# A fixed order of TensorE products, more reordered stretches, an fp32r second norm, a shared last multiplication and ten more low parts by accumulating transfers

## The chip, the core and the metric

The program runs on one core of a Trainium2 chip. A core has a matrix engine (PE; its weight loads are listed apart as PEld), a vector engine (DVE), an activation engine (ACT), a general engine (POOL), a sequencer that issues most transfers (SP), and sixteen DMA engines that move data between HBM and the on-chip memory. Each engine works through its own queue in order and waits on semaphores for the others. The metric is the time of one execution in microseconds (us) on the device, taken as the median of several runs.

## The reference: what is computed

Two request groups share all weights: one prompt of 256 tokens and 8 sequences of 4 new tokens, 288 columns in all. One layer is applied, then a last norm:

```python
def trunk_layer(x, ...):
    h = rmsnorm(x, norm1_g)
    proj = jnp.einsum("btd,de->bte", h, w_in) + b_in          # 2048 -> 3072
    a, gate, z = proj[..., :D_CONV], proj[..., D_CONV:2 * D_CONV], proj[..., 2 * D_CONV:]
    u = a * jax.nn.sigmoid(gate)
    c = jax.nn.silu(layernorm(depthwise_causal_conv(u_ext, conv_w, conv_b), ln_g, ln_b))
    d = multiscale_pool(z_ext, pos0)                          # windows 2, 4, 8, 16
    p = jnp.einsum("btgc,gce->btge", d, pool_w).reshape(bsz, T, D_POOL) * pool_scale
    mix = jnp.concatenate([c, p], axis=-1)
    x = x + jnp.einsum("btm,md->btd", mix, w_out)             # 2048 -> 2048
    h2 = rmsnorm(x, norm2_g)
    f = jnp.square(jax.nn.relu(jnp.einsum("btd,df->btf", h2, w_ff1)))   # 2048 -> 8192
    x = x + jnp.einsum("btf,fd->btd", f, w_ff2)               # 8192 -> 2048
    return x, u_ext[:, -(CONV_W - 1):], z_ext[:, -(POOL_MAX - 1):]
```

All arrays are float32. The outputs are the normed x of both groups and the last 30 values of `u` and the last 15 of `z` as new states.

## The kernel before

Channels lie on the 128 partitions, the 288 tokens along the free axis. Every float32 weight and every float32 activation is split into two fp32r numbers, a high part (a rounded copy) and a low part (what is left), and a product of two such numbers is taken as three TensorE products of 128x128 by 128x288: high by high, low weight by high activation, high weight by low activation. They are called products below. There are 8,112 of them and all stand at line 315.

**Weights.** A block is 1024 rows by 256 columns. SP loads it in two raw tiles `wr` of four 128-row slices each (512 KB). ACT casts a raw tile to the high part `whi` (line 265). The low part `wlo` is made in one of three ways (`split_part`, lines 259 to 273): V, DVE subtracts (line 270); G, POOL subtracts in two halves (line 273); D, ACT writes the negated high part into `wlo` (line 267) and POOL issues a transfer that reads the weights from HBM once more and adds them onto `wlo` (line 268). The table `WAYS` (line 73) says which way is taken, by stage, in turn for successive tiles. `whi` and `wlo` have five buffers each, `wr` six; a tile is cast when PE has let go of a buffer, and each tile serves 24 products.

**Stages.** `SEQUENCE` (line 45) gives the order of the input projection: `c0` to `c7` are the eight pairs of 128 channels of `a` and `gate` (96 products each; c0 and c1 are done together), `p3` to `p0` are the four pooling groups (96 each), `P3` to `P0` the products by `pool_w` (12 each). After each pair c, DVE does 30 multiply-adds of the convolution (line 434, `pc`), which keep it full from about 40 to 195 us; POOL does the window sums of each p (lines 466 to 475). `w_out` follows in two halves: first the rows of the pooling channels (`dx` tiles, 8 groups of 48 products, lines 553 to 559), in which between products the mean and the variance of the layer norm are taken, then the rows of the convolution channels (`mx` tiles, 8 groups of 48, lines 576 to 580). In the first half the activations are taken in the order of `korder`, so of a block's two tiles the second is used first. Then come four rounds of 8 groups of `w_ff1` (`ax` tiles, 96 products each) and 8 of `w_ff2` (`fx` tiles, 96 each).

**Order.** Tile, the layer under the kernel, runs its own estimate of the time line and lets an instruction that is ready pass one that is not, in each engine's queue, before the program is built. So the order of products on PE is that of the code only where the estimate sees no wait; `tc.issue_after` pins an order where it is used (lines 231, 314, 508, 555). Inside a group of products `gemm` (line 291) has a list `todo`; `classes`, where given, permutes its head: each product has a class, (k + part of the activation) mod 2, and the string says which class comes next. `TURN` (line 70) is such a string of 48. Without it the classes alternate. `TURN` is used in c2 and in the groups of index 2 of both halves of `w_out` and of the first round of `w_ff1`.

**Norms.** `rsqrt_sums` and `spread` (lines 221 to 251) reduce a row of sums over the partitions with six small float32 products into 96x3 numbers, take the inverse root there, and spread it back with three float32 products. The second norm's row `ss2` is summed up by POOL (line 604) from squares that ACT takes of each finished x (line 603), and is reduced behind the first group of `w_ff1` (line 615). At the end (lines 649 to 653) DVE multiplies the 16 rows of x by the last norm's row in six pieces, and SP sends each off.

Of the kernel before, what the change touches and what calls it, by code (L numbers as in the profile page):

```python
# [44 lines left out]
SEQUENCE = [(_s[0], int(_s[1])) for _s in "c0 c1 c2 c3 c4 p3 c5 p2 P3 c6 p1 P2 p0 P1 c7 P0".split()]  # L45
# [27 lines left out]
WAYS = {"c2": "GVGV", "c3": "GDGG", "c4": "GDGD", "p3": "GDDG", "c5": "GDGD", "c": "GGGV", "p": "GVVG", "w": "GG", "ff": "VV"}  # L73
# [13 lines left out]
def trunk_kernel(ctx: ExitStack, tc: tile.TileContext, io):  # L87
# [133 lines left out]
    def rsqrt_sums(parts, scale, after=None, busy=(0, 0)):  # L221
# [5 lines left out]
        idle = cvp.tile([P, 512], F32, name=nm("idle"), tag="cv") if sum(busy) else None  # L227
        for n, t in enumerate(parts):
            for j in range(3):
                last = nc.tensor.matmul(pt[:TB, j : j + 1], t[:, j * TB : (j + 1) * TB], ones[:, 0:1], start=n + j == 0, stop=n == len(parts) - 1 and j == 2)  # L230
            with tc.issue_after(last.ins):
                for j in range(busy[n] if n < 2 else 0):
                    nc.tensor.matmul(idle[:, 0:P], ones, ones, start=True, stop=True)  # L233
# [12 lines left out]
    def spread(sums):  # L246

        s, pr, _ = sums
        for j in range(3):
            last = nc.tensor.matmul(pr[:, j * TB : (j + 1) * TB], s[:, j : j + 1].to_broadcast([TB, P]), ident, start=j == 0, stop=j == 2)  # L250
        return pr, last

    def rsqrt_rows(*args):
        return spread(rsqrt_sums(*args))[0]

# [34 lines left out]

    def gemm(banks, rhs, m_outer=False, between={}, classes=""):
# [3 lines left out]
        gets = ready.pop()  # L295
        step = 2 if len(banks) == 2 else 1
        pairs = [(k, m) for k in range(0, n, step) for m in range(len(banks))]
        if m_outer:
            pairs.sort(key=lambda km: km[1])
        if step == 2:  # L300
            parts = ((0, 0, 0), (1, 0, 0), (0, 1, 0), (1, 1, 0), (1, 0, 1), (0, 0, 1))
        else:
            parts = ((0, 0, 0), (0, 0, 1), (0, 1, 0))
        todo = [(k + d, m, w, x) for k, m in pairs for d, w, x in parts]
# [407 lines left out]
```

## Time and profile before

| what | us |
|---|---|
| median of 3 runs (lowest, highest) | 1088.29 (1088.22, 1089.59) |
| the profiled execution | 1087.97 |
| its span, from first to last instruction | 1086.2 |
| PE busy | 1073.7 |
| DVE busy | 634.0 |
| ACT busy | 477.9 |
| POOL busy (nearly all of it before 207 us) | 182.7 |

The profiled execution lies 0.3 us under the median and 1.8 us over its own span. Times in the rows below are counted from the first instruction. PE is busy 99% of the span, so what it waits shows only as small gaps; busy time includes a product's own latency (292 ns each, overlapping its neighbours), and the rate at which products start has to be read from a count and the time it takes. In the chain of waits each row gives the start, the length, the engine and tile, and the number of instructions merged; in a time line the bracket at the end of a row tells how long the engine idled before it and what ended that.

### The profile page before, as it was taken

The numbers are of one execution on the slowest core, as the hardware profiler recorded it, in microseconds if no ns is written. First come the engines' busy times: TensorE is split into PE (matmuls) and PEld (weight loads), VectorE is DVE, ScalarE is ACT, GpSimd is POOL, SyncE is SP. The second block draws the span as 40 slices with busy tenths as digits, with TensorE's granted clock in tenths as the row PEclk, the third lists the DMA queues.
The fourth block names the chain that finished last, engine by engine and source line by source line (L and its number), as shares of the span: only waits on it lengthen the run. The fifth ranks groups of instructions, "written<-read, shape, count | busy, mean of one in ns | idle before, by whom it ended". The sixth has DMA issues, their size and how long they took to land.

```text
span 1086.2 us, 19609 instructions
## 1 busy us (share of the span) xinstructions
PE 1073.7 (99%) x8206; PEld 1071.4 (99%) x8206; DVE 634.0 (58%) x813; ACT 477.9 (44%) x583; POOL 182.7 (17%) x212
## 2 busy tenths in 40 slices
PE   9999999999999999999999999999999999999996
PEld 8999999999999999999999999999999999999996
DVE  7899999678555444445454444545544445554553
ACT  8654445475544433334443333444433334444441
POOL 0888989613000000000000000000000000000000
PEclk9999999999999999999999999999999999999998
DMA  9896467545455555555555555555555555555522
GB/s 333 281 269 177 136 178 245 183 153 178 159 171 169 164 172 174 166 167 173 167 167 172 172 165 168 175 167 165 174 169 165 172 173 165 167 174 166 168 76 88
DMA packets 58120, 190.71 MB, mean 176 GB/s; under 512 B 6192, under 2 KB 11312, under 8 KB 58032
## 3 DMA queue, kind: packets, MB, share of 16 engines
q1 hardware_dynamic: 56480, 185.27, 52.2%
q0 software_dynamic: 1008, 3.67, 1.9%
q8 instruction: 64, 1.05, 0.4%
q10 hardware_dynamic: 544, 0.52, 0.1%
q14 instruction: 24, 0.20, 0.0%
HBM read 185.16 MB, written 4.28 MB: 174 GB/s over the span
## 4 chain that ended last, share of the span: by engine, by line
PE 96%; DVE 1%; ACT 1%; DMA 1%; issue 1%; POOL 0%; DVEq 0%
PE ac L315 95%; DMA wr<-in_w 1%; PE pp L315 0%; DVE xT L652 0%; ACT whi L265 0%; DVE wlo L270 0%; POOL wlo L273 0%; PE idle L233 0%; ACT n L567 0%; PE pt L250 0%; PE pt L230 0%; DVE z_all L391 0%; ACT z_all L389 0%; ACT hx L340 0%; DVE n L564 0%
## 5 line engine op out<-in xcount | busy, mean ns | idle before, releaser
L265 ACT CAST whi<-wr 128x1024 fp32r<-128x1024 f32 (+1 forms) x341 | 356.6, 1046 | 558.4 <-PE ac L315 540.4
L270 DVE TENSOR_TENSOR wlo<-wr,whi 128x1024 fp32r<-128x1024 f32 (+1 forms) x295 | 362.9, 1231 | 350.3 <-ACT whi L265 350.3
L315 PE MATMUL ac<-ax,whi 128*128 128x288 f32 x2048 | 351.5, 292 | 0.0
L315 PE MATMUL ac<-fx,whi 128*128 128x288 f32 x2048 | 350.1, 292 | 0.0
L315 PEld LDWEIGHTS ac<-ax,whi 128*128 128x128 f32 x2048 | 296.2, 187 | 0.0
L315 PEld LDWEIGHTS ac<-fx,whi 128*128 128x128 f32 x2048 | 295.6, 187 | 0.0
L315 PE MATMUL ac<-ax,wlo 128*128 128x288 f32 x1024 | 217.4, 292 | 0.0
L315 PE MATMUL ac<-fx,wlo 128*128 128x288 f32 x1024 | 216.3, 292 | 0.0
L315 PEld LDWEIGHTS ac<-ax,wlo 128*128 128x128 f32 x1024 | 162.7, 187 | 0.0
L315 PEld LDWEIGHTS ac<-fx,wlo 128*128 128x128 f32 x1024 | 162.2, 187 | 0.0
L315 PE MATMUL ac<-hx,whi 128*128 128x288 f32 x768 | 136.3, 295 | 0.6 <-DVE hx L338 0.6
L315 PEld LDWEIGHTS ac<-hx,whi 128*128 128x128 f32 x768 | 113.8, 188 | 1.0 <-ACT whi L265 0.8
L273 POOL TENSOR_TENSOR wlo<-wr,whi 128x512 fp32r<-128x512 f32 x78 | 105.9, 1411 | 32.7 <-ACT whi L265 30.4
L434 DVE SCALAR_TENSOR_TENSOR pc<-u_all,vec,pc 128x256 f32<-128x256 f32 x232 | 99.8, 483 | 3.0 <-ACT pc L431 1.6
L315 PE MATMUL ac<-hx,wlo 128*128 128x288 f32 x384 | 86.1, 296 | 0.3 <-DVE wlo L270 0.2
L315 PEld LDWEIGHTS ac<-hx,wlo 128*128 128x128 f32 x384 | 62.7, 188 | 1.1 <-DVE wlo L270 0.9
L315 PE MATMUL ac<-dx,whi 128*128 128x288 f32 x256 | 46.1, 296 | 0.0
L315 PE MATMUL ac<-mx,whi 128*128 128x288 f32 x256 | 45.2, 294 | 0.1
L617 DVE SCALAR_TENSOR_TENSOR t<-ac,r 128x576 f32<-128x576 f32 x32 | 24.2, 758 | 26.3 <-PE ac L315 25.2
L315 PEld LDWEIGHTS ac<-mx,whi 128*128 128x128 f32 x256 | 37.5, 188 | 0.6 <-ACT mx L569 0.3
L315 PEld LDWEIGHTS ac<-dx,whi 128*128 128x128 f32 x256 | 38.0, 188 | 0.1
L646 DVE TENSOR_TENSOR xT<-xT,ac 128x576 f32<-128x576 f32 x24 | 18.1, 754 | 19.4 <-PE ac L315 19.4
(108 smaller groups left out, 502.9 us busy)
## 6 DMA issues: line engine op xcount, KB each, us to landing
wr<-in_w SPq DMA_DIRECT2D x335, 512.0 KB, 3.6
wlo<-in_w POOLq DMA_DIRECT2D x7, 512.0 KB, 7.3
xT<-in_xT SPq DMA_DIRECT2D x7, 288.0 KB, 6.6
out_u_out<-u_all SPq DMA_DIRECT2D x1, 1208.0 KB, 9.7
out_yT<-xT SPq DMA_DIRECT2D x2, 576.0 KB, 2.9
u_all<-in_hist_c SPq DMA_DIRECT2D x8, 136.0 KB, 5.2
wr<-in_w SPq DMA_DIRECT2D x4, 256.0 KB, 3.3
out_z_out<-z_all SPq DMA_DIRECT2D x1, 668.0 KB, 8.2
```

The lines of the kernel that those rows point to most:

```text
L265: nc.scalar.copy(hi, raw)
L270: nc.vector.tensor_tensor(lo, raw, f32(hi), op=ALU.subtract)
L273: nc.gpsimd.tensor_tensor(lo[:, j : j + 2, :], raw[:, j : j + 2, :], f32(hi[:, j : j + 2, :]), op=ALU.subtract)
L315: last = nc.tensor.matmul(banks[m][:, :T], gets[k // 8](k % 8, m)[w], rhs[k][x], start=j == ends[m][0], stop=j == ends[m][1])
L434: nc.vector.scalar_tensor_tensor(out=dst, in0=up[:, w : w + SEQ], scalar=cwv[:, w : w + 1], in1=pc, op0=ALU.mult, op1=ALU.add)
L617: nc.vector.scalar_tensor_tensor(out=t, in0=bk[:, :, :T], scalar=0.0, in1=both(r2), op0=ALU.max, op1=ALU.mult)
L646: nc.vector.tensor_tensor(x2, x2, bk[:, :, :T], op=ALU.add)
```

## The change

- **Order.** Every product from the end of c0/c1 to the third group of `w_ff1` is now issued through `mm`, which pins it behind the product before it (`chain`), so that PE's order is the order of the code there. `gemm` with four banks takes its k in pairs after the first two.
- **Sequence.** P1 is no longer a step of its own: its 12 products stand inside c7, after c7's first 48. P0 follows c7 directly.
- **Repeated reordering.** `TURN` is given to c0/c1, c2, c4 to c7, to groups 1 and 4 of both halves of `w_out`, and to group 1 of the first round of `w_ff1`.
- **Second norm.** The row `ss2` is split into high and low (ACT, DVE) and reduced by two fp32r products with a constant matrix, which also spread it; they stand inside the first group of `w_ff1`, after 24 of its 96 products. Square root, reciprocal and three more DVE operations then run on 128x288.
- **Last norm.** ACT takes the root straight from PSUM, four filler products stand for six, and the last multiplication is shared: DVE takes twelve rows in six pieces, reading the spread row in PSUM, POOL the last four one by one, from a copy that ACT makes. The pieces are sent by SP and ACT in turn.
- **Low parts.** `WAYS` gives way D to one more tile each of c6 and c7 and to the second tile of each of the eight blocks of the first half of `w_out`: ten in all, from G.
- The small load of `vec` goes ahead of the first x.

Three places in the built order, before and after. Names carry the program's numbers.

PE at the start of `w_ff1` (`ac30` is its first group in both; `ss2` the row of squares; `whi85`, `whi86` are that group's first two weight tiles). Before:

```order
L315 MATMUL ac30_3463<-ax7_3449,wlo88_3445 128x288
L315 MATMUL ac30_3463<-ax8_3450,wlo88_3445 128x288
L315 MATMUL ac30_3463<-ax8_3450,whi88_3444 128x288
L315 MATMUL ac30_3463<-ax7_3449,whi88_3444 128x288
L230 MATMUL pt3_3584<-ones_110,ss21_2865 96x1 x3
L315 MATMUL ac31_3606<-ax1_2928,whi89_3564 128x288 x2
```

After:

```order
L303 MATMUL ac30_3490<-ax2_3016,whi85_3371 128x288 x2
L303 MATMUL ac30_3490<-ax2_3016,wlo85_3372 128x288 x2
L303 MATMUL ac30_3490<-ax2_3016,whi85_3371 128x288 x4
L303 MATMUL ac30_3490<-ax2_3016,wlo85_3372 128x288 x2
L303 MATMUL ac30_3490<-ax2_3016,whi85_3371 128x288 x2
L303 MATMUL mean21_3518<-hl_3515,means_157 128x288 x2
L303 MATMUL ac30_3490<-ax3_3089,whi86_3375 128x288 x2
```

The reduction moved from behind the group's 96th product to behind its 24th.

PE at the start of the second half of `w_out` (`mx1` to `mx4` are the four tiles of normed convolution channels, `ac22` and `ac23` the first two groups). Before:

```order
L315 MATMUL ac22_2866<-mx1_2841,whi69_2828 128x288 x2
L315 MATMUL ac22_2866<-mx1_2841,wlo69_2829 128x288 x2
L315 MATMUL ac23_2937<-mx1_2841,whi71_2919 128x288 x2
L315 MATMUL ac23_2937<-mx1_2841,wlo71_2920 128x288 x2
L315 MATMUL ac22_2866<-mx1_2841,whi69_2828 128x288 x4
```

After:

```order
L303 MATMUL ac22_2883<-mx1_2858,whi69_2780 128x288 x2
L303 MATMUL ac22_2883<-mx1_2858,wlo69_2781 128x288 x2
L303 MATMUL ac22_2883<-mx1_2858,whi69_2780 128x288 x4
L303 MATMUL ac22_2883<-mx1_2858,wlo69_2781 128x288 x2
L303 MATMUL ac22_2883<-mx1_2858,whi69_2780 128x288 x2
L303 MATMUL ac22_2883<-mx2_2865,whi69_2780 128x288 x2
```

Before, the two groups alternate, 24 products on each `mx` tile; now the first group runs through all four tiles with 12 products on each before the second begins.

POOL in the first half of `w_out` (`wlo` low parts, `sum_c` the layer norm's sums, `prd8` products of the last convolution pair). Before:

```order
L438 TENSOR_TENSOR prd8_2253<-u_all_87,vec_85 128x8x31 x4
L273 TENSOR_TENSOR wlo58_2416<-wr58_2408,whi58_2415 128x512 x2
L273 TENSOR_TENSOR wlo59_2475<-wr59_2470,whi59_2474 128x512 x2
L443 TENSOR_TENSOR sum_c_242<-sum_c_242,c3_1066 128x288
L273 TENSOR_TENSOR wlo60_2480<-wr60_2472,whi60_2479 128x512 x2
L273 TENSOR_TENSOR wlo61_2539<-wr61_2534,whi61_2538 128x512 x2
```

After:

```order
L456 TENSOR_TENSOR prd8_2272<-u_all_87,vec_85 128x8x31 x4
L275 DMA wlo58_2371<-in_w 128x1024
L280 TENSOR_TENSOR wlo59_2430<-wr59_2425,whi59_2429 128x512 x2
L461 TENSOR_TENSOR sum_c_247<-sum_c_247,c3_1071 128x288
L275 DMA wlo60_2435<-in_w 128x1024
L464 TENSOR_TENSOR sum_c_247<-sum_c_247 128x288
L280 TENSOR_TENSOR wlo61_2494<-wr61_2489,whi61_2493 128x512 x2
```

Every second tile (even numbers, the one that its group uses first) now comes by transfer.

The diff, cut to its core:

```diff
-SEQUENCE = [... "c0 c1 c2 c3 c4 p3 c5 p2 P3 c6 p1 P2 p0 P1 c7 P0".split()]
+SEQUENCE = [... "c0 c1 c2 c3 c4 p3 c5 p2 P3 c6 p1 P2 p0 c7 P1 P0".split()]
+TURNS = ("c4", "c5", "c6", "c7")
...
-WAYS = {... "c": "GGGV", "p": "GVVG", "w": "GG", "ff": "VV"}
+WAYS = {... "c": "GDGV", "p": "GVVG", "w": "GD", "ff": "VV"}
...
+    nc.sync.dma_start(vec[:, 0:NG], io["vec"][:, 0:NG])
     for k, n in FIRST[:6]:
         first_x(k, n)
-        if k == 0:
-            nc.sync.dma_start(vec[:, 0:NG], io["vec"][:, 0:NG])
-        elif k > 1:
+        if k > 1:
             first_weights(k, n, nc.sync)
...
+    def inverse_root(mean, root, y, out):
+
+        nc.vector.reciprocal(y, root)
+        nc.vector.scalar_tensor_tensor(out=root, in0=mean, scalar=EPS, in1=y, op0=ALU.add, op1=ALU.mult)
+        nc.vector.scalar_tensor_tensor(out=root, in0=root, scalar=-0.5, in1=y, op0=ALU.mult, op1=ALU.mult)
+        nc.vector.scalar_tensor_tensor(out=out, in0=root, scalar=1.5, in1=y, op0=ALU.add, op1=ALU.mult)
...
+    chain = []
+
+    def mm(*args, **kw):
+
+        with tc.issue_after(chain[-1]) if chain else nullcontext():
+            last = nc.tensor.matmul(*args, **kw)
+        if chain:
+            chain[0] = last.ins
+        return last
...
-    with tc.issue_after(gemm(pair0 + pair1, hx, between={15: first_sums})):
-        third = conv_products(2, between={2: first_rows}, classes="01" * 18 + TURN)
+    chain.append(gemm(pair0 + pair1, hx, classes="010" * 4 + "101" * 4 + "01" * 24 + TURN))
+    third = conv_products(2, between={0: first_sums, 4: first_rows}, classes="01" * 15 + TURN)
...
+    def pool_between():
+
+        ready.extend(itertools.islice(weights, 1))
+        return pool_products(1)
+
     for kind, i in SEQUENCE[3:]:
         if kind == "c":
-            conv_pair(i, conv_products(i))
+            conv_pair(i, conv_products(i, between={8: pool_between} if i == 7 else {}, classes=TURN if f"c{i}" in TURNS else ""))
...
-        with behind:
-            last = gemm(each(bk), [mixp[k] for k in korder], between=BETWEEN.get(g, {}), classes=TURN if g == 2 else "")
-        behind = tc.issue_after(last) if g > 3 else nullcontext()
+        gemm(each(bk), [mixp[k] for k in korder], between=BETWEEN.get(g, {}), classes=TURN if g in (1, 4) else "")
...
-        gemm(each(bk), mixc, classes=TURN if g == 2 else "")
+        gemm(each(bk), mixc, classes=TURN if g in (1, 4) else "")
...
+    def second_rows():
+
+        hl = actp.tile([P, 4, T], F32R, name="hl", tag="act")
+        hi, lo = hl[:, 1, :], hl[:, 0, :]
+        nc.scalar.copy(hi, ss2)
+        nc.vector.tensor_tensor(lo, ss2, f32(hi), op=ALU.subtract)
+        bk, r2 = ms("mean2"), row("r2")
+        mean, root = bk[:, 0, :T], bk[:, 1, :T]
+        mm(mean, means, hi, start=True, stop=False)
+        last = mm(mean, means, lo, start=False, stop=True)
+        nc.scalar.activation(root, mean, AF.Sqrt, bias=eps)
+        inverse_root(mean, root, r2, r2)
...
-            gemm(each(bk), x1, classes=TURN if ch == 0 and g == 2 else "")
-            if ch == 0 and g == 0:
-                nc.scalar.copy(r2, rsqrt_rows([ss2], 1.0 / D))
+            gemm(each(bk), x1, between={4: second_rows} if ch == 0 and g == 0 else {}, classes=TURN if ch == 0 and g == 1 else "")
+            if ch == 0 and g == 2:
+                chain.clear()
...
-    rf = rsqrt_rows([ssf, qf], 1.0 / D, None, (3, 6))
-    for k0, n in ((0, 1), (1, 2), (3, 4), (7, 4), (11, 3), (14, 2)):
-        xk = xT[:, k0 : k0 + n, :]
-        nc.vector.tensor_tensor(xk, xk, rf[:, None, :T].to_broadcast([P, n, T]), op=ALU.mult)
-        nc.sync.dma_start(io["yT"][:, k0 : k0 + n, :], xk)
...
+    queues = (nc.sync, nc.scalar)
+
+    def finish(eng, r, pieces):
+
+        for j, (k0, n) in enumerate(pieces):
+            xk = xT[:, k0 : k0 + n, :]
+            eng.tensor_tensor(xk, xk, r[:, None, :].to_broadcast([P, n, T]), op=ALU.mult)
+            queues[j % 2].dma_start(io["yT"][:, k0 : k0 + n, :], xk)
+
+    finish(nc.vector, rows_f, ((0, 1), (1, 1), (2, 2), (4, 2), (6, 3), (9, 3)))
+    nc.scalar.copy(rf, rows_f)
+    finish(nc.gpsimd, rf, [(k, 1) for k in range(12, KT)])
```

In the built order ACT's queue ends with the root, three issues of the last DVE pieces (of one, two and three rows), then the copy `rf`, then two issues of POOL's rows. P1's 12 products stand on PE between the 48th and 49th of c7.

More of the change, by code (lines that the diff above doesn't have):

```diff
@@ L309, in gemm @@
         ends = {m: [f(j for j, p in enumerate(todo) if p[1] == m) for f in (min, max)] for m in range(len(banks))}
[L310 removed]
         for j, (k, m, w, x) in enumerate(todo):
[L312 to L315 removed]
+            if begins.get(j) in between:
+                between[begins[j]]()
+            last = mm(banks[m][:, :T], gets[k // 8](k % 8, m)[w], rhs[k][x], start=j == ends[m][0], stop=j == ends[m][1])
         ready.extend(itertools.islice(weights, 1))
@@ L491, in pool_products @@
             mixp[i] = (mh, ml)
+        return last
     for i in range(2):
```

80 lines of the change are left out of this document (48 added, 32 removed).

## The prediction

> **What bounds the kernel now.** First the page's list of engines:
>
> ```profile
> PE 1073.7 (99%) x8206; PEld 1071.4 (99%) x8206; DVE 634.0 (58%) x813; ACT 477.9 (44%) x583; POOL 182.7 (17%) x212
> ```
>
> PE is never idle for long, so the time is the number of products times the distance between their starts, plus the few waits. The distance comes from the table of windows (start and end, length, PE busy with its instructions, granted clock, DMA share, GB/s):
>
> ```profile
> 85.00:109.00 24.00, 24.00 (x182) 1.00 0.59 171
> 242.00:270.00 28.00, 28.00 (x218) 1.00 0.55 183
> 310.00:1070.00 760.00, 760.00 (x5849) 1.00 0.50 163
> 1072.00:1086.20 14.20, 3.81 (x35) 0.78 0.42 167
> ```
>
> Some two products already run when a window opens, so I take two from each count: 24.00/180 = 133.3 ns, 28.00/216 = 129.6, 760/5847 = 130.0. There are two gaits at the same full clock, 3.3 ns apart. The chain of waits (start, length, engine and tile) shows how little else there is:
>
> ```profile
> 164.75 1.30 POOL wlo L273
> 166.10 3.71 PE ac L315 x26
> ...
> 220.70 63.42 PE ac L315 x480
> 284.12 0.43 PE pt L230 x6
> ...
> 290.24 0.64 PE pt L250 x6
> 290.88 781.06 PE ac L315 x6006
> ```
>
> The reader is to see that 6,006 of 8,112 products stand in one unbroken run of 781.06 us (130.0 ns each), and that the change touches what lies ahead of it and the end. Every microsecond that PE waits there is lost whole, since nothing later has slack to give it back.
>
> **The change part by part.** Sums go against the profiled execution, 1087.97 us; the median lies 0.3 above it.
>
> *Reordered stretches.* They remove no product. The slow window lies in c5 to p0, the fast ones behind the group that has `TURN` already. If the string brings the fast gait from c5's on, the 456 products from there to p0's end gain 456 x 3.3 ns = 1.5 us. The other new strings lie where the gait is fast already or where I expect waits to break it. The ends are 0 and, for about 1,100 slow products of the front (that window's gait up to the one at 242), -3.6. I take -1.5. The small load placed ahead of the first x I leave at 0 (+-0.3): it is 8 KB.
>
> *P1 inside c7.* Its 12 products now stand 48 products, 6.3 us, behind p0's last. The way to its operands before:
>
> ```profile
> 151.57 0.75 DVE L457 TENSOR_TENSOR tz<-ac,rb 128x576 f32<-128x576 f32 x1
> ...
> 156.89 0.79 POOL L475 TENSOR_TENSOR d<-s,z_all 128x32 f32<-128x32 f32 x1
> ...
> 157.71 0.68 ACT L477 CAST dx<-d 128x576 fp32r<-128x576 f32 x1 [2.33 <-POOL d L475]
> ...
> 159.44 0.75 DVE L478 TENSOR_TENSOR dx<-d,dx 128x576 fp32r<-128x576 f32 x1
> ```
>
> This is the last window sum that P1 and P0 wait for in the row of steps. p0's products end shortly before 151.57, say 151.5; the high part is there 6.9 us later (158.39), the low part 8.7 (160.19), of which DVE spends one on convolution pieces that stand first. PE comes at 6.3 and is served at 7.9 to 8.7: a wait of 1.6 to 2.4. Before, P1 had waited for nothing, but a POOL low part cost some 0.3 there:
>
> ```profile
> L315 PEld LDWEIGHTS ac<-dx,wlo 128*128 128x128 f32 x128 | 20.9, 188 | 0.4 <-POOL wlo L273 0.3
> ```
>
> It goes. Net +1.3 (-0.3 if POOL, relieved of low parts, is early enough; 2.1 at most).
>
> *Ten low parts by transfer.* Each takes POOL's two halves of a subtraction away and adds an ACT pass, a POOL issue and 512 KB of traffic. Rows of the seven that exist, then one cast in the first half of `w_out` and the group end behind which its products come, then the two state outputs and the issue of the larger one:
>
> ```profile
> L268 POOL DMA_DIRECT2D wlo<-in_w x7: 817/875/1169, 42.4 to 83.8; - x7
> ...
> DMA to landing us min/median/max: 5.8/7.3/10.1
> ```
>
> ```profile
> L267 ACT ACTIVATE wlo<-whi 128x1024 fp32r<-128x1024 f32 x7 | 7.4, 1058 | 0.1
> ```
>
> ```profile
> 183.81 1.05 ACT L265 CAST whi<-wr 128x1024 fp32r<-128x1024 f32 x1 [2.29 <-PE ac L315]
> ```
>
> ```profile
> 193.08 0.75 DVE L559 TENSOR_TENSOR xT<-xT,ac 128x576 f32<-128x576 f32 x1 [0.89 <-PE ac L315]
> ```
>
> ```profile
> out_u_out<-u_all SPq DMA_DIRECT2D x1, 1208.0 KB, 9.7
> ...
> out_z_out<-z_all SPq DMA_DIRECT2D x1, 668.0 KB, 8.2
> ```
>
> ```profile
> 172.26 0.55 SPq L522 DMA_DIRECT2D out_u_out<-u_all  x1
> ```
>
> From cast to use lie 193.08 - 183.81 = 9.3 us, and the cast cannot come earlier, since it waits for PE to free a buffer. Needed are 1.05 (cast) + 1.06 (second pass) + 0.3 (an allowance for the semaphores until POOL issues) + 5.8, 7.3 or 10.1 = 8.2, 9.7 or 12.5 us: 1.1 early, 0.4 late or 3.2 late. All eight in `w_out` are the tiles that their group uses first. PE waiting here also holds the casts behind it, so a wait lengthens the next tile's lead; they do not simply add. The state outputs leave ahead of and beside the first groups (the larger at 172.26, one or two tiles before the cast shown) and load the engines more than what stood beside the seven. I price two tiles at half the longest shortfall (3.2), the rest at 0.3 together: +3.5. Ends: 0 (all as the quickest) and eight times 0.4 plus 14.8 from four late ones, 18. The Trainium skill ("DMA: Bandwidth & Descriptors", section on the anatomy of a SWDGE transfer) gives about 2.0 us + bytes/436e3 for such a transfer, by which 512 KB would take an estimated 3.2 us and this term would be 0; the seven rows here, accumulating ones, do not agree (5.8 at least), and the rows decide.
>
> *Second half of w_out.* Its first two groups alternated; now the first alone needs all four `mx` tiles, and the second follows. What feeds the fourth, and the second group's end:
>
> ```profile
> 225.27 1.15 ACT L567 ACTIVATE n<-n,vec 128x288 f32<-128x288 f32 x2
> 226.53 1.06 ACT L265 CAST whi<-wr 128x1024 fp32r<-128x1024 f32 x1
> 227.48 0.67 ACT L569 CAST mx<-n 128x576 fp32r<-128x576 f32 x1
> ```
>
> ```profile
> 228.76 0.76 DVE L570 TENSOR_TENSOR mx<-n,mx 128x576 fp32r<-128x576 f32 x1
> ...
> 234.11 0.75 DVE L580 TENSOR_TENSOR xT<-xT,ac 128x576 f32<-128x576 f32 x1 [0.31 <-PE ac L315]
> ```
>
> The fourth tile is whole at 228.2 and 229.5 (about 228.8 where DVE takes it at once). PE started at 220.70 and has 36 products for the three tiles ahead, done by 225.5 at the soonest: it stands until 228.8, does what is left of the first group by 229.9, and then 48 products x 131 ns, to 236.2. Before, both groups were done 0.2 before 234.11. +2.3; +0.5 if the chain of the norm starts earlier, +3 if the fourth tile comes at 229.5.
>
> *Second norm.* The fp32 pieces of the chain, 0.43 and 0.64, go; two products (0.26) come, after 24 products of the group:
>
> ```profile
> 271.48 0.42 PE L315 MATMUL ac<-ax,whi 128*128 128x288 f32 x2
> ```
>
> ```profile
> 273.64 2.00 POOL L604 TENSOR_TENSOR ss<-ss,q 128x288 f32<-128x288 f32 x2 [4.23 <-ACT q L603]
> ```
>
> ```profile
> 274.80 1.06 ACT L265 CAST whi<-wr 128x1024 fp32r<-128x1024 f32 x1 [0.53 <-PE ac L315]
> ```
>
> ```profile
> 275.89 1.23 DVE L270 TENSOR_TENSOR wlo<-wr,whi 128x1024 fp32r<-128x1024 f32 x1
> ```
>
> ```profile
> L543 DVE TENSOR_TENSOR q<-q 128x288 f32<-128x288 f32 x1 | 0.5, 459 | 0.0
> ...
> L615 ACT COPY r<-pt 128x288 f32<-128x288 f32 x1 | 0.4, 400 | 1.9 <-PE pt L250 1.9
> ```
>
> PE is there at 271.48 + 24 x 0.13 = 274.6. The row of squares is whole at 275.64; ACT's copy follows its cast (275.86 + 0.40 = 276.3), DVE's subtraction its own (277.12 + 0.46, by the row of `q`, = 277.5). PE waits 2.9, and all products are pinned behind. 2.9 + 0.26 - 1.07 = +2.1; +0.7 if ACT and DVE take the row first, +3 if they are late. What comes after the root on 128x288 has the group's other 72 products, 9.4 us, to hide in.
>
> *The end.* ACT sends three of DVE's pieces and waits for each in its queue; its copy for POOL stands behind the last. So POOL's four rows begin after DVE's twelve, not beside them.
>
> ```profile
> 1075.85 5.28 DVE L652 TENSOR_TENSOR xT<-xT,pt 128x288 f32<-128x288 f32 x6 [1.00 <-PE pt L250]
> ```
>
> ```profile
> L604 POOL TENSOR_TENSOR ss<-ss,q x15: 817/911/1732, 235.7 to 274.7; 128x288 f32<-128x288 f32 x15
> ```
>
> ```profile
> 1074.31 0.16 DVE L241 TENSOR_TENSOR st<-st 96x3 f32<-96x3 f32 x1
> ```
>
> ```profile
> 0.72 0.98 ACTq L184 DMA_DIRECT2D wr<-in_w  x2
> ```
>
> ```profile
> DMA to landing us min/median/max: 1.8/2.9/3.8
> ```
>
> DVE's end was 1081.13. Sixteen rows took 5.28, so twelve take 4.1 in as many pieces; two small steps like the one of 0.16, with their hops, fall out of the root (-0.35). DVE is done at 1079.6, then an issue on ACT (0.98 for two, 0.5) and the copy (0.40), and POOL's four rows of 0.82 to 1.0 end at 1083.8 to 1084.5: +3.0. The last transfer was 1 of 2 rows, and is now 1 of 1 row, some 1.6 shorter by the landings of the outputs (1.8 for the one row sent before, up to 3.8). +1.4 (0.7 to 2.3).
>
> Sum: -1.5 + 1.3 + 3.5 + 2.3 + 2.1 + 1.4 = +9.1, so 1087.97 + 9.1 = 1097.1 on the profiled execution, about 1097 as a median too.
>
> **The rivals.** *A, the transfers are in time*, as their quickest row has it: without 3.5, 1093.5. For it, POOL no longer queues anything ahead of the issues; against it, the two outputs. *B, the waits take each other's place.* A later PE finds the convolution, the norm's row and P1 ready, and the string gives all of the front the fast gait: 9.1 less 1.3, 2.3 and 2.1, and 2.1 more gain: 1089, no change. Against it: the second half of `w_out` and the second norm hang on PE's own products, so they move with it. *C, the long run loses its gait.* A wait ahead of `w_ff1` leaves PE at 133.3, and the string of group 1 does not mend it: 6006 x 3.3 = +20 us, 1117. Every fast window here stands behind such a string, so the chance is small. *D, the clock falls behind a wait.* The last window, with PE busy for 3.81 of 14.20 us, has a clock of 0.78, all others 1.00; if each of three waits of 2 to 3 us costs as much again, 1103. The Trainium skill ("TensorE: Matmul & The Clock Gate", Part 1) lets the clock fall after an idle window of about 3.4 us, by which these waits would just not do it; no row here tells. *E, the other side: faster.* The string repeated may bring a third gait, as far under 130.0 as that lies under 133.3: 126.7 ns over the run of 6,006, -20 us, 1077. It decides from (9.1 + 2.2)/6006 = 1.9 ns per product. Against it, the window from 310 to 1070 us is behind such a string already and shows 130.0. The skill's same page (section on the back-to-back gap) has N/2.4 + 2.5 ns, an estimated 122.5 ns for 288 columns, which the trace does not reach. Smaller, on the same side: all terms at their low ends (-3.6, -0.3, 0, 0.5, 0.7, 0.7) give 1086, just past the bound below.
>
> **How the numbers follow.** The forecast has a chance of 0.52, A 0.15, B 0.10, C 0.04, D 0.06, E 0.05, the low ends together 0.08. What a measurement of this kernel can tell from no change is about 0.2%, 2.2 us. Slower: forecast, A, C, D = 0.77; same: B = 0.10; faster: E and the low ends = 0.13. The range leaves out E, most of the low ends and C, and the upper part of the transfers' term: 1087 to 1103. The forecast's own is 1092 to 1103.
>
> **What would show it.** The profile after should have a window of c6 and p0 at 130 ns; a PE gap of 1.6 us ended by DVE `dx` inside c7; gaps ended by the transfers in the first groups of `w_out`, near 180 us; one of 3 us ended by DVE `mx` after 225; one of about 3 ended by DVE's low part of the row of squares 24 products into `w_ff1`; the long run at 130.0; and POOL's four rows behind DVE's twelve. It is wrong if the long run has another gait, if transfers land in over 12 us, or if the gaps are there singly but not together.

## The result, and the profile after

The changed kernel takes 1104.57 us (median of 4 runs, 1103.57 to 1107.27) against 1088.26 before (1087.80 to 1089.59): a ratio of 1.0152, 95% interval 1.0130 to 1.0174. It is 16.3 us slower. Forecast were about 9 us, with a range up to 1103. The sign was right, the size was not, and the time lies outside the range. The profiled execution (1105.53, 1.0 above the median) has a span of 1103.8 us, 17.6 more than before.

First the engines of the changed kernel, then its table of what PE waited for (who waited, for whom, us in total, times, longest):

```profile
PE 1077.5 (98%) x8192; PEld 1072.4 (97%) x8192; DVE 631.5 (57%) x815; ACT 486.4 (44%) x594; POOL 167.5 (15%) x206
```

```profile
PE ac L303 <- DMA wlo<-in_w: 6.9, 4, 3.9
PE mean L303 <- ACT hl L635: 1.5, 1, 1.5
...
PE ac L303 <- ACT mx L591: 0.9, 2, 0.6
PE mean L303 <- DVE hl L636: 0.9, 1, 0.9
PE ac L303 <- DVE mx L592: 0.7, 1, 0.7
```

The largest wait is for low parts that come by transfer. The chain of waits has the three late ones:

```profile
163.65 9.22 DMA wlo<-in_w
...
180.46 8.87 DMA wlo<-in_w
...
195.04 7.83 DMA wlo<-in_w
```

PE starts again as each of them lands (in the bracket, how long it idled):

```profile
172.91 0.53 PE L303 MATMUL ac<-dx,wlo 128*128 128x288 f32 x2 [3.88 <-DMA wlo<-in_w]
...
189.37 0.40 PE L303 MATMUL ac<-dx,wlo 128*128 128x288 f32 x1 [1.95 <-DMA wlo<-in_w]
...
202.91 0.40 PE L303 MATMUL ac<-dx,wlo 128*128 128x288 f32 x1 [0.63 <-DMA wlo<-in_w]
```

The fourth wait of that row of the table, 0.4 us, is for c7's low part by transfer, at 154.7 us.

The windows (start and end, length, PE busy and instructions, granted clock, DMA share, GB/s) show what the waits alone don't:

```profile
140.00:150.00 10.00, 10.00 (x80) 1.00 0.53 154
172.00:182.00 10.00, 9.09 (x57) 0.83 1.08 284
...
290.00:296.00 6.00, 5.89 (x33) 0.72 0.25 87
310.00:1070.00 760.00, 760.00 (x5848) 1.00 0.52 167
```

The long run has the gait it had before (760/5846 = 130.0 ns), and the window at 140 us is fast too. But after the wait that ends at 172.9 us, and after the second norm's two products at 290 us, PE is nearly always busy and does few products: 57 in 10 us. The granted clock is down (a cold clock, below), and products start 240 ns apart instead of 130. In the trace these are 14 products behind the first wait and 11 behind the norm.

To account for the whole, the start of the same product by count is compared in the two traces. Lengths of the stretches, us:

| stretch (numbers of products) | before | after | difference | forecast |
|---|---|---|---|---|
| start, to the 188th | 32.27 | 32.89 | +0.6 | 0 |
| to the 1048th, the gait | 114.57 | 113.46 | -1.1 | -1.5 |
| to the 1201st, c7 with P1 | 20.68 | 22.25 | +1.6 | +1.3 |
| to the 1585th, first half of `w_out` | 53.18 | 62.18 | +9.0 | +3.5 |
| to the 1729th, second half's first groups | 19.58 | 21.99 | +2.4 | +2.3 |
| to the 1969th, the rest of that half | 31.20 | 31.30 | +0.1 | |
| to the 2205th, second norm | 32.25 | 35.60 | +3.4 | +2.1 |
| to the 8112th, the long run | 767.92 | 767.92 | 0.0 | 0 |
| tail, from there to the span's end | 14.55 | 16.21 | +1.7 | +1.4 |

The differences sum to 17.6 before rounding. Each column is one trace: in a second trace of the kernel before (last experiment) the second stretch takes 117.0 us, 2.1 of them a wait for one of its seven transfers at 63 us, and all kernels with the change take 113.5 to 114.0 there.

### The profile page after: what moved, and what is told of

The parts are those of the page before. It is cut to its first block, busy times and chain, and to the rows that moved or that the text cites. A ratio compares the mean times of both kernels' runs of the same rounds, so it can differ in the third digit from the quotient of the medians.

```text
span 1103.8 us, 19604 instructions
## 1 busy us (share of the span) xinstructions
PE 1077.5 (98%) x8192; PEld 1072.4 (97%) x8192; DVE 631.5 (57%) x815; ACT 486.4 (44%) x594; POOL 167.5 (15%) x206
## 4 chain that ended last, share of the span: by engine, by line
PE 69%; issue 21%; DVE 4%; DMA 3%; POOL 2%; ACT 1%; SPq 0%; POOLq 0%; DVEq 0%; ACTq 0%
PE ac L303 68%; DMA wlo<-in_w 2%; DVE pc L452 2%; DMA wr<-in_w 1%; DVE wlo L277 1%; POOL wlo L280 1%; POOL s L484 0%; ACT whi L272 0%; POOL xT L708 0%; ACT n L589 0%; PE pt L303 0%; POOL prd L456 0%; DVE z_all L409 0%; PE pp L303 0%; DVE tz L475 0%
## 5 line engine op out<-in xcount | busy, mean ns | idle before, releaser
L708 POOL TENSOR_TENSOR xT<-xT,rf 128x288 f32<-128x288 f32 x4 | 3.0, 790 | 808.8 <-ACT rf L712 808.8
L280 POOL TENSOR_TENSOR wlo<-wr,whi 128x512 fp32r<-128x512 f32 x58 | 78.9, 1392 | 40.1 <-ACT whi L272 39.3
## 6 DMA issues: line engine op xcount, KB each, us to landing
out_u_out<-u_all SPq DMA_DIRECT2D x1, 1208.0 KB, 12.5
```

Of the source, the lines that this page charges most:

```text
L280: nc.gpsimd.tensor_tensor(lo[:, j : j + 2, :], raw[:, j : j + 2, :], f32(hi[:, j : j + 2, :]), op=ALU.subtract)
L708: eng.tensor_tensor(xk, xk, r[:, None, :].to_broadcast([P, n, T]), op=ALU.mult)
```

## The experiments

Theories: L, every wait counts at its length, since nothing behind it gives time back, and a cold clock behind the longest counts besides. W, the waits only stand in for others. Each edit is against the changed kernel unless another base is named.

### Low parts by subtraction again

```diff
-WAYS = {... "c": "GDGV", "p": "GVVG", "w": "GD", "ff": "VV"}
+WAYS = {... "c": "GDGV", "p": "GVVG", "w": "GG", "ff": "VV"}
```

> The changed kernel with the eight tiles of the first half of w_out subtracted by POOL again (the two more transfers in c6 and c7 stay). Theory L (late transfers, and a cold clock behind the longest of them): the changed kernel's trace has three waits for these transfers, 4.18, 2.24 and 0.92 us from start to start less 0.13 each, together 6.9, and 14 product starts 240 ns apart behind the first, 110 ns each too much, 1.5. Without them the kernel is 8.4 us faster than the changed one, about 1096. Rival W (the waits only stand in for others: the convolution on DVE and the layer norm behind it would be waited for anyway): 3 to 4 us faster at most, about 1101, with a new gap ahead of the second half of w_out.

Measured: 1096.26 us, 8.3 less than the changed kernel. The first half of `w_out` takes 53.07 us, as it did before the change (53.18). W falls: nothing took the place of these waits. The 9.0 us of that stretch belong to the eight transfers.

### The same transfers on the tile used second

```diff
-WAYS = {... "w": "GD", ...}
+WAYS = {... "w": "DG", ...}
```

> The changed kernel with the same number of transfers, but in each block of c6, c7 as they are and of w_out for the other of the two tiles, the one that its group uses second. Theory L: 24 products, 3.1 us, more from cast to use, so that a transfer has some 10 us to land instead of 6.9; with the landings of 7 to 10 us seen, at most 1 us of waits is left: 7 us faster than the changed kernel, about 1097.5. Rival T (the accumulating transfers themselves load the engines until they are late wherever they stand): landings beyond 10 us and gaps of 3 us or more, less than 4 us faster, 1101 or more.

Measured: 1095.70 us, 8.9 less. What PE waits for in this kernel:

```profile
PE mean L303 <- ACT hl L635: 1.5, 1, 1.5
PE ac L303 <- ACT whi L272: 1.2, 1, 1.2
...
PE ac L303 <- DMA wlo<-in_w: 0.3, 1, 0.3
```

Of 6.9 us for transfers 0.3 are left, and these are for c7's low part at 154 us; the eight of `w_out` make PE wait for nothing, with landings no shorter (median 8.5 us). The 1.2 us for ACT's cast lie in the start. So the transfers are not too many or too heavy. They were given to the tile with 24 products less lead.

### The second norm 24 products later

```diff
-            gemm(each(bk), x1, between={4: second_rows} if ...)
+            gemm(each(bk), x1, between={8: second_rows} if ...)
```

> The changed kernel with the second norm's two products after 48 instead of 24 products of the first group of w_ff1. Theory L with the cold clock: the two waits (1.76 and 1.30 us from start to start, less 0.26 of their own) and the 12 starts at 240 ns behind them (1.3) both go: 4.1 us faster than the changed kernel, about 1100.5. Rival N (the slow starts come with the norm itself, not with the wait): 2.8 us faster, and 240 ns intervals behind the two products at their new place. Rival M (the rest of the norm now comes late for the first group's end): a new gap at the second or third group.

Measured: 1100.70 us, 3.9 less. The stretch of the norm takes 31.03 us, 4.6 less than in the changed kernel and 1.2 less than before the change: without the wait the fp32r reduction is the gain that it can be.

This run's trace also has a case of its own in the first half of `w_out`: a wait of 1.90 us with a cold clock behind it.

```profile
188.90 0.40 PE L303 MATMUL ac<-dx,wlo 128*128 128x288 f32 x1 [1.90 <-DMA wlo<-in_w]
```

```profile
189.00:194.00 5.00, 5.00 (x27) 0.66 0.99 262
```

### Useless products in the norm's wait

```diff
+        fill = cvp.tile([P, 512], F32, name="fill", tag="cv")
+        for j in range(6):
+            mm(fill[:, 0:P], ones, ones, start=True, stop=True)
         mm(mean, means, hi, start=True, stop=False)
+        for j in range(4):
+            mm(fill[:, 0:P], ones, ones, start=True, stop=True)
```

> The changed kernel with six float32 products of 128x128 with no use ahead of the second norm's first product and four ahead of its second, so that PE is busy where it waited; the operands come no earlier. Theory L with the cold clock: the waits stay as long as they were, but the 12 starts at 240 ns behind them are 130 ns again: 1.3 us faster than the changed kernel (1.0 to 1.6), about 1103.2. Rival N (the slow starts follow the kind of product, not the idle time): the 240 ns stay, and the time is that of the changed kernel or 0.3 longer.

Measured: 1104.35 us, 0.2 less, which is within the spread of the changed kernel's own runs. The trace decides. The norm's stretch takes 34.16 us instead of 35.60, and PE's window over it stays at full clock:

```profile
284.00:290.00 6.00, 5.87 (x48) 1.00 0.52 175
```

So the slow starts cost 1.4 us in the changed kernel; the waits beside them stayed. The time did not show it, since in this trace 20 products instead of 14 were slow behind the first transfer.

One such trace alone does not show that the useless products did it. Four other traces have the same two waits of the norm, 1.5 and 0.9 us. The changed kernel has 11 slow products behind them, the run with the low parts by subtraction 24 (stretch 36.76 us), and the runs with the tiles exchanged and with the states late (below) none (34.16 us each). So a gap of this length costs a cold clock in one execution and not in another:

```profile
278.00:288.00 10.00, 7.64 (x35) 0.66 0.34 105
```

```profile
278.00:288.00 10.00, 7.63 (x56) 1.00 0.34 105
```

The first is the run with the low parts by subtraction, the second that with the tiles exchanged: PE was busy equally long, with 35 and 56 instructions.

The traces tell what it goes by. In all seventeen the granted clock changes only at whole multiples of 3.413 us from its first change, so each trace falls into stretches of that length. Three of the changed kernel that hold a long wait, each with the stretch behind it:

```profile
170.47:173.88 3.41, 0.96 (x7) 1.00 1.04 344
173.88:177.29 3.41, 3.41 (x16) 0.50 1.05 266
187.53:190.95 3.42, 1.58 (x12) 1.00 1.01 313
190.95:194.36 3.41, 3.41 (x28) 1.00 0.97 252
286.52:289.93 3.41, 1.23 (x8) 1.00 0.50 157
289.93:293.34 3.41, 3.23 (x13) 0.50 0.45 154
```

The views count what runs in a stretch. By the products that start in it, over some 5,300 stretches of the seventeen traces ahead of the tail, half clock came behind each of the eleven with at most 11 starts and behind no other. The wait of 1.95 us at 187 us left 12 starts in its stretch, one of 1.97 us with the states late left 11. So it goes by how much of a gap falls into one stretch, which differs from execution to execution. The norm's stretch of this run:

```profile
286.91:290.32 3.41, 3.28 (x27) 1.00 0.46 154
```

Twenty of its 27 instructions are the useless products (two for each float32 product); without them it would be one of the low ones. This was read off the traces afterwards; no run was made to test it, and 11 and 12 are counts of products of 288 columns in these traces alone.

### Both repairs, as a base

Low parts of the first half of `w_out` by subtraction, and the norm after 48 products, with the edits above.

> The changed kernel with both repairs at once: POOL subtracts the low parts of the first half of w_out, and the second norm's two products stand after 48 products. Theory L: the two gains lie in different places and both are lost time of PE, so they add: 8.3 + 3.9 = 12.2 us faster than the changed kernel, about 1092.4; no product starts at 240 ns behind a wait. Rival: a part of one gain is eaten by a later wait, 1094 to 1096. It serves the next three as their base.

Measured: 1091.74 us, 12.8 less than the changed kernel. The gains add, and the trace has no slow products behind a wait.

### The second half's first groups unpinned (on the base)

```diff
+        if g == 0:
+            chain.clear()
-        gemm(each(bk), mixc, classes=TURN if g in (1, 4) else "")
+        last_m = gemm(each(bk), mixc, classes=TURN if g in (1, 4) else "")
+        if g == 1:
+            chain.append(last_m)
```

> The base of the last run, and the first two groups of the second half of w_out not pinned, so that they alternate again. Theory O (the pinned order costs the difference between standing for the fourth normed tile with 48 products still to do and with few to do): 2.2 us faster than the base, about 1090.2, and the gaps of 0.9, 0.65 and 0.9 us in front of the second to fourth tile are gone or shorter. Rival: the layer norm's own chain on ACT and DVE sets when the tiles come, and the end of the second group is the same: within 0.5 us of the base.

Measured: 1089.34 us, 2.4 less than the base. The two groups alternate again and the stretch takes 19.75 us (base 21.93, before 19.58). The pinned order is the cause.

### The start and P1 (on the base)

```diff
-    nc.sync.dma_start(vec[:, 0:NG], io["vec"][:, 0:NG])
     for k, n in FIRST[:6]:
         first_x(k, n)
-        if k > 1:
+        if k == 0:
+            nc.sync.dma_start(vec[:, 0:NG], io["vec"][:, 0:NG])
+        elif k > 1:
...
-            conv_pair(i, conv_products(i, between={8: pool_between} if ...))
+            conv_pair(i, conv_products(i, between={12: pool_between} if ...))
```

> The base, with two things undone at places that the trace tells apart: the small load of vec behind the first x again, and P1's 12 products inside c7 after 72 products instead of 48. Theory V (the first x comes later because the small load stands ahead of it): the 192nd product starts at 31.3 us instead of 32.4 to 32.8, 1.1 us. Rival R (the new order of the products of c0 and c1 costs it, since it asks for the weights of a pair of rows at once): the 192nd product starts where it did. For P1, theory L: its two waits of 0.4 to 0.8 and 0.65 us go, about 1.0 us; rival: another wait takes their place at P0 or at the first group of w_out. Both theories: 2.1 us faster than the base, about 1090.3.

Measured: 1091.34 us, 0.4 less than the base: neither part did what was expected. The start was no earlier (188th product at 34.61 us in this trace), but this trace cannot judge the load: PE has a cold clock from 12.4 to 15.9 us, so that 14 products start 240 ns apart.

```profile
12.45:15.85 3.40, 3.40 (x16) 0.50 1.03 374
```

P1 waits for nothing now, but P0, which follows it, does, and the stretch of c7 takes 22.26 us as in the base (22.30). The table of waits has nearly the same sizes as before the move (0.4 for ACT, 0.3 for DVE in the changed kernel), now in front of P0:

```profile
PE pp L304 <- ACT dx L496: 0.5, 1, 0.5
...
PE pp L304 <- DVE dx L497: 0.4, 1, 0.4
```

### The copy ahead of the issues (on the base)

```diff
+    nc.scalar.copy(rf, rows_f)
     finish(nc.vector, rows_f, ((0, 1), (1, 1), (2, 2), (4, 2), (6, 3), (9, 3)))
-    nc.scalar.copy(rf, rows_f)
     finish(nc.gpsimd, rf, [(k, 1) for k in range(12, KT)])
```

> The base, with ACT's copy of the last norm's row ahead of ACT's issues of DVE's pieces, so that POOL's four rows run beside DVE's twelve. Theory Q (the copy's place in ACT's queue puts POOL's rows last): POOL's rows end 4 us earlier, before DVE's; 3.0 to 4.0 us faster than the base, about 1089. Rival S (the two engines slow each other, or the transfers set the end): POOL's rows take 1.5 us each or DVE's twelve rows 6 us, and less than 1.5 us is gained.

Measured: 1089.84 us, 1.9 less than the base; 3 to 4 were expected. The tail takes 13.93 us instead of 15.76. First the base, then this kernel, in the time line:

```profile
1078.67 4.08 DVE L708 TENSOR_TENSOR xT<-xT,ends 128x288 f32<-128x288 f32 x6 [1.00 <-PE ends L700]
...
1083.64 3.04 POOL L708 TENSOR_TENSOR xT<-xT,rf 128x288 f32<-128x288 f32 x4 [803.87 <-ACT rf L712]
```

```profile
1078.74 4.08 DVE L708 TENSOR_TENSOR xT<-xT,ends 128x288 f32<-128x288 f32 x6 [1.43 <-ACT rf L711]
1078.78 3.06 POOL L708 TENSOR_TENSOR xT<-xT,rf 128x288 f32<-128x288 f32 x4 [799.38 <-ACT rf L711]
```

POOL's rows start 4.9 us earlier, and neither engine slows the other (4.08 and 3.04 to 3.06 us in both). Of the gain, 0.4 goes to DVE's wait for the copy (1.43 instead of 1.00), and the work now ends with DVE's last row at 1082.8 instead of POOL's at 1086.7. From there the transfers take 5.3 us to the span's end, 3.6 in the base. They all leave within 4 us now, and land in up to 4.4 us instead of 2.7.

### The state outputs after the transfers

The two outputs are sent by SP behind the raw weights of the second half's first groups (`sp_last` holds the last load issued so far).

```diff
-    with later(2 * LATER):
-        nc.sync.dma_start(io["u_out"], u_all[:, :, UO - CH : UL])
-        nc.sync.dma_start(io["z_out"], z_all[:, :, ZO - PH : ZL])
...
-            nc.sync.dma_start(*raw[-1])
+            sp_last[:] = [nc.sync.dma_start(*raw[-1]).ins]
...
         gemm(each(bk), mixc, classes=TURN if g in (1, 4) else "")
+        if g == 1:
+            with tc.issue_after(sp_last[0]), later(2 * LATER):
+                nc.sync.dma_start(io["u_out"], u_all[:, :, UO - CH : UL])
+                nc.sync.dma_start(io["z_out"], z_all[:, :, ZO - PH : ZL])
```

> The changed kernel with the two state outputs sent behind the raw weights of the first groups of the second half of w_out, so that they do not lie beside the ten accumulating transfers of c6, c7 and the first half of w_out. Theory C (the outputs make the transfers late): landings of 6 to 7 us for the transfers issued between 160 and 200 us, the three waits gone but for 1 us, and no cold clock there: 7 us faster than the changed kernel, about 1097.5. Rival T (an accumulating transfer beside the steady loads of raw weights lands in 8 to 9 us anyway, and the lead of 9.3 us is too short): the waits stay at 4 to 7 us, less than 3 us faster.

Measured: 1101.03 us, 3.5 less than the changed kernel, between the two theories. The table of waits and the landings:

```profile
PE ac L304 <- DMA wlo<-in_w: 2.9, 3, 2.0
```

```profile
DMA to landing us min/median/max: 5.6/7.7/10.2
```

Of 6.9 us of waits 4.0 belong to the outputs; 2.9 remain beside the steady loads alone. The first of them, 1.97 us, has 13 slow products behind it:

```profile
173.00:177.00 4.00, 4.00 (x21) 0.58 0.99 245
```

### Four repairs together, with two variants of them

The low parts by subtraction, the norm after 48 products, the unpinned groups and the copy ahead; then the same with the old order of the first products; then the first of these with the two more transfers in c6 and c7 given back to POOL:

```diff
-            units[:1] = [(0, 1), (1, 1)]
+            units = [(k, 1) for k in range(n)]
...
-    chain.append(gemm(pair0 + pair1, hx, classes="010" * 4 + "101" * 4 + "01" * 24 + TURN))
+    chain.append(gemm(pair0 + pair1, hx))
```

```diff
-WAYS = {... "c": "GDGV", ...}
+WAYS = {... "c": "GGGV", ...}
```

> The changed kernel with four parts mended together: POOL subtracts in the first half of w_out, the norm after 48 products, the first two groups of the second half alternating, the copy of the last row ahead of the issues. Each alone gave 8.3, 3.9, 2.4 and 1.9 us; if they add, about 1087.4 to 1088, 1 us faster than the kernel before. Rival: the start, 1.1 us later than before, eats it: same as before.

> The last kernel, with the products of c0 and c1 in the order of the kernel before (one row of weights after another, no class string). Theory R (the order by pairs of rows asks for the second row's weights and x before they are there): the 192nd product starts at 31.3 instead of 32.2 to 32.8 us, 1.1 us faster than the last kernel, about 1086.5. Rival: the transfers at the start are what is late, and the order of products changes nothing: within 0.3 us.

> The second kernel of this call (four parts mended), with the two more transfers in c6 and c7 given back to POOL. Theory: those two have more lead and cost PE nothing, and POOL is behind at 150 to 165 us, so giving the work back to POOL brings a wait of 0.5 to 1.5 us there: slower by that. Rival: the wait of 0.6 to 1.1 us in front of a low part at 154 us in the changed kernel belongs to them, and goes: faster by 0.5 to 1.

Measured: 1087.72 us with the four (ratio to the kernel before 0.9997, 0.9988 to 1.0007), 1087.54 with the old first order (0.9994, 0.9981 to 1.0006). The four gains add up to the kernel before, and not beyond. From the 48th to the 192nd start on PE, counted with the warming products ahead, the new first order takes 20.3 to 20.4 us (21.1 in the trace with the cold clock in the start) and the old one 19.8 to 19.9 in all traces here; it costs about 0.5. The medians, 0.2 apart, cannot show that.

Without the two transfers in c6 and c7 the time is 1091.66, 3.9 us more, where 0.5 to 1.5 were expected. POOL's backlog then falls on P1, and 12 products behind the two waits start 240 ns apart, which is 1.3 of the 3.9 us:

```profile
PE pp L303 <- ACT dx L495: 2.4, 1, 2.4
PE pp L303 <- DVE dx L496: 1.6, 1, 1.6
```

So of the ten new transfers the two in c6 and c7 are a gain of 3.9 us where P1 stands so early, though PE waits 0.3 to 1.7 us for c7's in every trace that has it, and the eight in `w_out` are a loss of 8.3.

### The whole start undone, P1 moved, and the kernel before once more

The first adds the load of `vec` in its old place to the old first order; the second moves P1 to after 72 products besides.

> The kernel with the four parts mended and the old order of c0 and c1, and with the small load of vec behind the first x again, so that the start is that of the kernel before in both respects. Theory B (order and load together set the start): the 192nd product starts at 31.3 us and the time is 0.5 to 1 us less than with the order alone, about 1086.8. Rival K (the start's transfers land as they happen to, from run to run): the 192nd product anywhere from 31 to 34 us, and the median within 0.5 us of the last kernel's 1087.5.

> The last kernel with P1's products after 72 instead of 48 products of c7. The trace of an earlier run showed that P1 then waits for nothing and P0 waits 1.2 us instead. Theory M (POOL's backlog sets when the last of the window sums is there; the wait only moves): the same time as the last kernel within 0.5 us. Rival: with less to wait for at the first place the transfer and the sum get ready by the second, 1 us faster.

> The kernel before once more, unchanged, for a second trace of it. Rival K for the start has the 192nd product anywhere from 31 to 34 us; theory B has it at 31.3 again within 0.3. Time 1088.3.

Measured: 1087.40, 1087.80 and 1088.28 us. The 188th product starts at 32.09 with the whole start undone, and in the second trace of the kernel before (an execution of 1091.82 us, 3.5 above the median) at 33.66 against 32.27 in the first. So about 1.4 us of the start differ from execution to execution, which covers the 0.6 of the table. Of the start only the 0.5 by order is shown, by the traces; the load of `vec` shows no effect. P1's place is worth nothing either way: 0.4 more, with the wait at P0 again.

The kernel with the whole start undone has a ratio of 0.9980 (0.9968 to 0.9991) to the kernel before. The kernel before itself, measured once more beside it, has 0.9986 (0.9971 to 1.0000), so two measurements of one kernel differ by 0.7 us (1088.94 and 1088.28). The 0.9 us from 1088.28 to 1087.40 are hardly more; a version that beats the kernel before is not shown.

## Why the prediction was right or wrong

- **What bounds the kernel.** Right. The long run kept its 130.0 ns, and the sum of what is lost ahead of it and behind it is the whole difference. "Every microsecond that PE waits there is lost whole" held in each experiment but P1's.
- **The gait.** Right: -1.1 where -1.5 was taken, and the window at 140 us is fast (10.00/78 = 128 ns). The two traces of the kernel before take 114.6 and, less a wait, 114.9 us, those with the change 113.5 to 114.0.
- **P1.** The size came out (+1.6 against +1.3) partly by luck, and the picture did not. P1's own two waits are worth 1.1 us from start to start; 0.6 of the stretch is the wait for c7's low part by transfer, which the step did not have, and 0.2 fell away at the first low part of `w_out`. That was POOL's old 0.3: the row quoted for it has `ac<-dx`, a product of `w_out`, not P1's `pp<-dx`. It went, and at the same product the first late transfer is waited for now. The step also took one chain of rows for what P1 and P0 both wait for, and so would have had the wait vanish 24 products later. It went over to P0 in two runs. What it hangs on is POOL's backlog, as the 3.9 us suggest that come when POOL gets two more subtractions.
- **Low parts by transfer.** This step failed: +3.5 was taken, +9.0 measured, more than half of the miss. The mechanism stood there: 9.3 us of lead from the cast, 9.7 needed with a median landing, 12.5 with the longest, and the tile used first in its group; that the state outputs slow the landings was named too, and they make up 4.0 of the 6.9 us. But the term was priced as "two tiles at half the longest shortfall". Of the eight in `w_out` three were late, by 4.05, 2.11 and 0.79 us from start to start, 6.95 together. The second and third had the lead that was forecast (9.6 and 9.5 us from the cast, 6.8 and 7.1 from issue to where PE came for them). The first had 7.7 from the cast and 5.2 from the issue, against a landing of 9.2. A further 1.5 us (14 products at 110 ns too much) is the cold clock, which this step did not have at all; some 0.5 us of the stretch stay unassigned. The term's upper end does not come out of its parts either: four shortfalls of 3.2 make 12.8, not 14.8. The range left that part out, so nothing else hangs on it.
- **The rule of the Trainium skill set beside it** ("DMA: Bandwidth & Descriptors", section on the anatomy of a SWDGE transfer), by which the transfers would land in an estimated 3.2 us and the term be 0, did not hold for these transfers: 5.6 us is the shortest of seventeen, 8.0 the median.
- **Second half of `w_out`.** Right in size (+2.4 against +2.3) and cause, as the unpinned groups show. The place was partly wrong: not one gap of 3 us before the fourth tile but three smaller ones, before the second, third and fourth.
- **Second norm.** The wait was right: 1.5 and 0.9 us idle where 2.9 between starts was forecast, the first ended by ACT's high part, the second by DVE's low part. The term was mis-sized, +3.4 against +2.1, by the 1.4 us of cold clock that the trace with the useless products does not have.
- **The end.** Right: +1.7 against +1.4, POOL's rows behind DVE's.
- **Rival D, the falling clock,** had a chance of 0.06, and was the second cause of the miss, together with the transfers. It was priced at three waits of 2 to 3 us; it came behind two, with 1.5 and 1.4 us. It was given little because no row told, which is no evidence against it.
- **The range** reached six us above the forecast, of which the transfers' term at its measured size uses up 5.5 alone. The cold clock was counted as a case apart; it came with the waits, and the two are not independent.
- **Other rivals.** A, B and E did not happen; C did not either: behind the norm's wait products start 133.3 ns apart, and 130.0 again behind the string of group 1.

## What to carry to other kernels

A transfer that a busy queue must feed in time is priced by its lead from issue to use against the whole spread of its landings, tile by tile: here the leads were 5.2 to 11.1 us and the landings 7.6 to 10.1, and three of eight came late. Of two tiles in a block, the slow way belongs to the one used second: that alone took 6.6 of 6.9 us of waits away. A PE wait of about two microseconds, or two shorter ones close together, can have a second price, the cold clock behind it. With a pinned order PE waits for every operand that is late.

## What the runs showed of the hardware

Idle time on PE was followed by a granted clock of 0.50, at which products start 240 ns apart, after gaps of 3.9, 3.5, 1.97 and 1.90 us, and after P1's 2.4 and 1.6 us where POOL has two more subtractions. It was not after gaps of 1.95 us in the changed kernel, 1.97 us in the second trace of the kernel before and 1.74 us in the run with the old first order; after 1.5 and 0.9 us with one product between it was in two traces of four. The clock changed only in steps of 3.413 us, and fell to 0.50 after the stretches with at most 11 starts. It stayed low for one or two such steps, 11 to 24 products, so such a gap cost 1.2 to 2.6 us more than its length. In the one trace with useless products in the gap it stayed at 1.00. The Trainium skill ("TensorE: Matmul & The Clock Gate", section "What's actually happening") has half rate after an idle window of about 3.4 us. The half rate agrees with 240 ns (by the page's 1.2 GHz, an estimated 288/1.2); an idle gap of that length was not needed here, since 1.90 and 1.97 us sufficed.

The accumulating transfers of 512 KB landed in 5.4 to 10.5 us over all runs, where plain loads of the same size have a median of 3.6 in the changed kernel's trace. POOL's multiplication of one row took 0.79 us on average, less than its additions of the same size in the kernel before, 0.82 to 1.73.
